# A hybrid SSD and latent-attention step: the query projection turned round, with tables for the rotation

## The chip, the cores and the metric

The kernel runs on one core of one Trainium2 chip. The metric is the time of one execution on the device in microseconds. A core has five engines that run side by side: TensorE (PE in the profile, with its weight loads listed apart as PEld), VectorE (DVE), ScalarE (ACT), GpSimd (POOL) and SyncE (SP), which here issues most DMA transfers. PE multiplies a stationary operand (up to 128x128, loaded first) with a moving one (up to 512 columns) and writes to PSUM, which DVE and ACT read; the other operands lie in SBUF, 128 partitions wide. DRAM is reached by DMA.

## The reference

One step of a two-layer decoder trunk: a Mamba-2 layer, then a multi-head latent attention layer (MLA), each added to the residual, and a final norm. There are 1024 prompt tokens and 64 sample tokens (8 sequences of 8 with a paged cache of 2048 positions), 1088 in all. What matters here is how the queries come about in the MLA layer:

```python
cq = rms_norm(proj[..., :o1], q_norm_w)              # 512 wide
q = jnp.einsum('btq,qhe->bthe', cq, w_uq)            # 16 heads, 64 + 32 wide
q_nope = q[..., :MLA_QK_NOPE]
q_pe = apply_rope(q[..., MLA_QK_NOPE:], cos[:, None, :], sin[:, None, :])

def apply_rope(x, cos, sin):
    x1, x2 = xf[..., :half], xf[..., half:]          # half = 16
    return jnp.concatenate([x1 * cos - x2 * sin, x2 * cos + x1 * sin], axis=-1)
```

Each head of the prompt then attends causally to 1024 keys of width 96 (64 made from the latent by `w_uk`, 32 rotated and common to all heads). The sample tokens do it in the latent space: `q_nope` is multiplied by `w_uk` (`absorb`), and the 256 wide result meets the cached latents directly.

## The kernel before

Values are float32. A matrix product of full accuracy is made of three products: each operand is split into a high part, rounded to the type that PE multiplies fast, and a low part (`split`, L127 and L133: ACT casts, DVE subtracts), and high x high, high x low and low x high are summed in PSUM.

The order of the work on the engines: most of the kernel is written as a program and put in order for every engine ahead of time by a planner that simulates the timeline. In the head loop and the sample stage the orders of PE and POOL are as written; DVE, ACT and SP are still planned. `issue_after(x)` tells the planner to put an instruction behind x. Each engine takes its instructions strictly in its order, SP its DMAs too.

The parts that the change and the prediction touch:

- `mla_cq` (ends at L1124) makes the normed query latent of nine token tiles (eight of 128 tokens, one of 64 with the sample tokens), turned so that the latent index lies on partitions: `cqh`, `cql`, four blocks of 128 by tokens. For the sample tile the low part goes beside the high one in `cqh`, so that one matmul of 128 weight columns takes both.
- `mla_q` (L1127 to L1155) is the query projection. The columns of `w_uq` are taken in four groups c of 384 (four heads of 96), loaded and split into `wqh`, `wql` by `load_w` (L318 is its DMA). For each group, nine token tiles: the latent is stationary (128 tokens) and the weight moves (384 columns), 12 matmuls (8 for the sample tile) into one of two PSUM buffers of tag pj (L98). ACT copies the result to `qt` (L1144; `fold`, L109 and L110, for the sample tile), DVE turns the rotary part in place with four operations (L1150 to L1153) and a DMA stores 192 KB to `q_d` in DRAM, tokens by columns (L1154). So there are 36 tiles, 32 of 128 tokens.
- `layer_mla` mixes 39 early units into those 36 tiles from the tenth on: the values and keys of the first heads (`vp`, `kp`, L86), queries of heads 0 and 1 (`prep_q`) and the score maxima of head 0 (`maxpass`).
- `mla_heads` is the loop over 16 heads: in head h, 12 blocks of scores st (`qk`, L1408 to L1415), two exponentials each (L1419, L1420, once rounded and once full), their difference tl on DVE or POOL in turn (L1422), and the product with the values o (`pv`, L1439 to L1441) two blocks later. Between the blocks stand, in a fixed merge, the maxima of head h + 1 (`sc`, L1376 to L1396, with a round trip through DRAM at L1395 and L1396) and the preparation of head h + 2 (keys, values, `prep_q`).
- `prep_q(h)` (L1319 to L1358): `load_q` fetches the queries of a pair of heads with tokens on partitions, 768 KB and 48 KB (L1316, L1317), a pair ahead from the third pair on. PE then turns them: one transpose for the 64 sample tokens (L1331), two of the raw key weight of this head (L1333), all in one PSUM tile `qs`; DVE and ACT copy out `qsn` (L1336) and `wt` (L1340) and split the sample's rotary part. Then twice four transposes of 128 tokens (`qT`, L1348) and a split from PSUM into the head's `qTh`, `qTl`. Last the two matmuls of `absorb` (`ql`, L1354) and their split.

Of the kernel before, what the change touches and what calls it, by code (L numbers as in the profile page):

```python
# [8 lines left out]
F32 = mybir.dt.float32  # L9
# [8 lines left out]
SEQ = 1024  # L18
# [977 lines left out]
def mla_in(k, right, mid):  # L996
    tc, nc, I = k.tc, k.nc, k.I
    k.g_d = k.dram.tile([8, 128, T], F32, name="g_d")
    with ExitStack() as st:
        xp = st.enter_context(open_pool(tc, name="hT", bufs=1))  # L1000
        k.xh = xp.tile([128, 8, T + 64], F32R, name="hh")
        k.xl = xp.tile([128, 8, T], F32R, name="hl")

        rw = st.enter_context(open_pool(tc, name="rw", bufs=1))
        sg = ExitStack()
        wg = sg.enter_context(open_pool(tc, name="wpg", bufs=1))
        with k.h0, open_pool(tc, name="h1", bufs=1, side="right") as p0:
# [23 lines left out]
        k.cqh = hp.tile([128, 4, T + 64], F32R, name="cqh")  # L1031
        k.cql = hp.tile([128, 4, SEQ], F32R, name="cql")
# [12 lines left out]
        k.wu0 = load_w(k, wu, I["mla_w_uq"][0].rearrange("q h e -> q (h e)")[:, :384], 4, 384, "wq", 1, None, 1)  # L1045
        mla_cq(k, sp, wcq)


# [54 lines left out]
def mla_cq(k, sp, ws):  # L1103
    nc = k.nc
    for i, (t0, m) in enumerate(TILES):
# [18 lines left out]
        split(k, k.cqh[:, :, t0 : t0 + m], k.cqh[:, :, T:] if m == 64 else k.cql[:, :, t0 : t0 + m], qs[:, :, :m])  # L1124


def mla_q(k, st):  # L1127
    tc, nc, I = k.tc, k.nc, k.I
    wuq = I["mla_w_uq"][0].rearrange("q h e -> q (h e)")
    wp = st.enter_context(open_pool(tc, name="wpq", bufs=1, side="right"))  # L1130
    sp = st.enter_context(open_pool(tc, name="spq", bufs=1, side="right"))
    ct, sn = k.rope
    for c in range(4):
        cs = slice(384 * c, 384 * c + 384)
        wh, wl = load_w(k, wp if c % 2 else k.wu, wuq[:, cs], 4, 384, "wq", 1, k.wu, 1) if c else k.wu0
        for i, (t0, m) in enumerate(TILES):
            qt = sp.tile([128, 4, 96], F32, tag="qt", name=f"qt{c}{i}", bufs=2)
            qf = qt.rearrange("p h e -> p (h e)")
            p = k.psum.tile([128, 512], F32, tag="pj", name=f"pq{c}{i}", bufs=PB["pj"])
            drain(mm_tok(nc, p, m, 384, [(*both(k.cqh, k.cql, i, kk), wh[:, kk], wl[:, kk]) for kk in range(4)]))  # L1140
            if m == 64:
                fold(nc, qf, p, 384)
            else:
                nc.scalar.copy(qf[:m], p[:m, :384])  # L1144
            u = sp.tile([128, 4, 2, 16], F32, tag="u3", name=f"u3{c}{i}", bufs=2)
            w = sp.tile([128, 4, 2, 16], F32, tag="w3", name=f"w3{c}{i}", bufs=2)
            cb = bass_bcast2(ct[:m, i], 4, 2)
            sb = bass_bcast2(sn[:m, i], 4, 2)
            pe = qt[:m, :, 64:96].rearrange("p h (a e) -> p h a e", a=2)
            nc.vector.tensor_tensor(u[:m], pe, cb, op=ALU.mult)  # L1150
            nc.vector.tensor_tensor(w[:m], pe, sb, op=ALU.mult)
            nc.vector.tensor_tensor(pe[:, :, 0], u[:m, :, 0], w[:m, :, 1], op=ALU.subtract)
            nc.vector.tensor_tensor(pe[:, :, 1], u[:m, :, 1], w[:m, :, 0], op=ALU.add)  # L1153
            nc.sync.dma_start(k.q_d[t0 : t0 + m, cs], qf[:m])  # L1154
            yield  # L1155


class Heads:
    def __init__(self, k, st):
# [10 lines left out]
        self.ones_rows(0)  # L1170
        self.add_k(vp, 1)
        self.ones_rows(1)
        self.qT, self.qts = [], {}
        self.add_q(vp, 0)
        self.add_q(vp, 1)

# [131 lines left out]
                    split(k, kh[0:64, cs], kl[0:64, cs], p[64 * jj : 64 * jj + 64])  # L1308
                yield

    def load_q(self, pr):
        k, nc = self.k, self.k.nc
        qt = self.sp.tile([128, 9, 192], F32, tag="qp", name=f"qp{pr}", bufs=2 if pr else 1)
        src = k.q_d[:, 192 * pr : 192 * pr + 192]
        with k.tc.issue_after(k.lastq.ins) if pr > 1 else nullcontext():
            nc.sync.dma_start(qt[:, :8], src[:SEQ].rearrange("(i p) e -> p i e", p=128))  # L1316
            nc.sync.dma_start(qt[:64, 8], src[SEQ:])  # L1317
        self.qts[pr] = qt

    def prep_q(self, h):  # L1320
        k, nc, sp = self.k, self.k.nc, self.sp
        hg, pr, j = h // 4, h // 2, h % 2
        if j == 0 and pr < 2:
            self.load_q(pr)
        if j == 1 and 0 < pr < 7:
            self.load_q(pr + 1)
        qt = self.qts[pr]
        if h == 2:
            nc.gpsimd.memset(self.qT[2][1][96:98].bitcast(F32), 0.0)
        p = self.wt(f"qs{h}")  # L1330
        nc.tensor.transpose(p[:96, :64], qt[:64, 8, 96 * j : 96 * j + 96], k.ident[:64, :64])  # L1331
        for c in range(2):
            nc.tensor.transpose(p[:64, 128 + c * 128 : 256 + c * 128],  # L1333
                                self.wkr[:, c, 64 * (h % 4) : 64 * (h % 4) + 64], k.ident)
        qsn = sp.tile([64, 64], F32, tag="qsn", name=f"qsn{h}", bufs=2)
        nc.vector.tensor_copy(qsn, p[:64, :64])  # L1336
        qv = k.qpr[:, :, NT * h : NT * h + NT]
        split(k, qv[0:32], qv[64:96], p[64:96, :64].rearrange("p (b t) -> p b t", t=NT))
        wt = sp.tile([64, 256], F32, tag="wt", name=f"wt{h}", bufs=2)
        nc.scalar.copy(wt, p[:64, 128:384])  # L1340
        yield
        if 1 < h < 4:
            self.ones_rows(h)
        qh, ql = self.q_of(h)
        for c in range(2):
            p = self.wt(f"qT{h}{c}")
            for i in range(4):
                nc.tensor.transpose(p[:96, i * 128 : i * 128 + 128], qt[:, 4 * c + i, 96 * j : 96 * j + 96], k.ident)  # L1348
            cs = slice(512 * c, 512 * c + 512)
            split(k, qh[:96, cs], ql[:96, cs], p[:96])  # L1350
            yield
        pl = self.wt(f"ql{h}p")
        for c in range(2):
            nc.tensor.matmul(pl[:, c * 64 : c * 64 + 64], wt[:, c * 128 : c * 128 + 128], qsn,  # L1354
                             start=True, stop=True)
        src = pl[:, :128].rearrange("p (c b t) -> p c b t", c=2, t=NT)
        split(k, *(x[:, :, :, NT * h : NT * h + NT] for x in (k.qlh, k.qll)), src)
# [40 lines left out]
    def qk(self, h, qc, jb):  # L1398
# [18 lines left out]
        tl = sp.tile([128, 512], F32R, tag="tl", name="tl", bufs=3)  # L1417
        P = sp.tile([128, 512], F32, tag="P", name="P", bufs=3)
        nc.scalar.activation(th[:, :n], ps[:, :n], AF.Exp, scale=SCALE)  # L1419
        nc.scalar.activation(P[:, :n], ps[:, :n], AF.Exp, scale=SCALE)  # L1420
        eng = nc.gpsimd if jb % 2 else nc.vector
        eng.tensor_tensor(tl[:, :n], P[:, :n], th[:, :n].bitcast(F32), op=ALU.subtract)  # L1422
        return th, tl
# [553 lines left out]
def layer_mla(k):  # L1977
# [1 line left out]
    k.og_d = k.dram.tile([8, 128, SEQ], F32, name="og_d")  # L1979
    k.npool = k.I["cache_ckv"].shape[1]  # L1980
    with ExitStack() as st:
        k.q_d = k.dram.tile([T, MH * 96], F32, name="q_d")
# [40 lines left out]
def consts():  # L2023
# [10 lines left out]
    ang = (pos[:, None] * inv[None, :]).astype(np.float32).reshape(9, 128, ROPE // 2).transpose(1, 0, 2)  # L2034
    c["c_cos"] = np.ascontiguousarray(np.cos(ang))
    c["c_sin"] = np.ascontiguousarray(np.sin(ang))
    m = np.where(i[None, :] <= i[:, None], 0.0, NEG).astype(np.float32)
    c["c_maskn"] = np.ascontiguousarray(np.concatenate([m, m.T], 1))
    c["c_slot"] = (i % 32).astype(np.float32)[:, None]
# [40 lines left out]
```

## Time and profile before

| what | value |
|---|---|
| median of 3 runs (lowest, highest) | 1924.01 us (1922.32, 1925.89) |
| the profiled execution | 1926.24 us |
| its span, first to last instruction | 1924.4 us |
| mean granted clock of TensorE | 0.997 |
| query projection (first and last pq matmul of `mla_q`) | about 1222 to 1313 us |
| head loop | from there to about 1620 us |
| DMA over the span | 202.02 MB, mean 105 GB/s |

How to read the profile's rows. A group row has the line, the engine, the operation, the output and inputs by their names in the program, the shape, the count, and then busy time, mean time of one, idle time of the engine just ahead of them and what ended it. The row of one tile's view has shortest, median and longest duration of one in ns instead, and the first and last start. A row of the chain is a start, a length and the work that stood on the path to the end then. Matmuls are pipelined: the duration of one is longer than the step from one to the next, and a busy PE need not be at its peak. Lines are those of the kernel before.

### The profile page before, as it was taken

How to read it: one execution, taken by the hardware profiler on the slowest of the kernel's cores; microseconds unless marked ns; L12 is line 12 of the kernel's file. 1: busy time of each engine (PE TensorE's matmuls, PEld its weight loads, DVE VectorE, ACT ScalarE, POOL GpSimd, SP SyncE). 2: the span in 40 equal slices, each digit the busy share in tenths (PEclk: the TensorE clock that was granted, in tenths of full speed). 3: DMA queues.
4: the chain of work that ended last, by engine and by line, in shares of the span. 5: the costliest groups of instructions: out<-in, count | busy, mean ns of one | idle time of the engine just before them, and what ended most of it. 6: DMA issues, size and time to landing. Idle time of an engine off the chain costs nothing.

```text
span 1924.4 us, 33639 instructions
## 1 busy us (share of the span) xinstructions
PE 1890.9 (98%) x12023; PEld 1728.8 (90%) x12023; DVE 1206.0 (63%) x2500; ACT 1102.0 (57%) x2523; POOL 823.3 (43%) x1122
## 2 busy tenths in 40 slices
PE   8999999999999999999999999999999999899998
PEld 7999999999999999888788998998888888788887
DVE  5557676757676757665534114567877888766674
ACT  6467566667666666733214314436777777755552
POOL 2447555545654555443004222104433435774551
PEclk9999999999999999999999999999999999999999
DMA  5223323333333232645534343123111112754541
GB/s 165 53 78 91 96 79 98 86 104 86 97 83 98 85 98 81 212 152 175 164 109 129 114 163 87 63 102 96 49 47 41 52 41 60 207 185 150 156 129 39
DMA packets 181087, 202.02 MB, mean 105 GB/s; under 512 B 18828, under 2 KB 147608, under 8 KB 180536
## 3 DMA queue, kind: packets, MB, share of 16 engines
q1 hardware_dynamic: 175864, 180.08, 30.9%
q0 software_dynamic: 4976, 19.66, 3.2%
q8 instruction: 95, 1.56, 0.4%
q14 instruction: 72, 0.59, 0.1%
q10 hardware_dynamic: 80, 0.13, 0.0%
HBM read 146.52 MB, written 53.28 MB: 104 GB/s over the span
## 4 chain that ended last, share of the span: by engine, by line
PE 84%; ACT 4%; DVE 4%; DMA 4%; issue 2%; POOL 1%; SPq 0%; POOLq 0%; DVEq 0%; ACTq 0%
PE pj L86 22%; PE pz L98 7%; PE pq L98 6%; PE pob L98 5%; PE p L98 5%; PE poa L98 3%; PE py L637 2%; PE sc L86 2%; PE o L86 2%; PE sc L1376 2%; PE o L1439 2%; PE o L1441 2%; PE st L1408 2%; PE st L1409 2%; PE st L1410 2%
## 5 line engine op out<-in xcount | busy, mean ns | idle before, releaser
L86 PE MATMUL pj<-xl,wih 128*128 128x384 f32 (+1 forms) x768 | 255.4, 333 | 0.0
L86 PE MATMUL pj<-xh,wih 128*128 128x384 f32 (+1 forms) x768 | 252.9, 333 | 1.2 <-ACT xh L273 0.9
L86 PE MATMUL pj<-xh,wil 128*128 128x384 f32 (+1 forms) x768 | 252.9, 329 | 0.0
L1422 POOL TENSOR_TENSOR tl<-P,th 128x384 fp32r<-128x384 f32 (+1 forms) x96 | 90.5, 942 | 234.3 <-ACT P L1420 192.7
L525 DVE SCALAR_TENSOR_TENSOR acc<-raw,vec,acc 128x1112 f32<-128x1112 f32 x96 | 140.9, 1469 | 14.9 <-ACT acc L521 14.0
L86 PEld LDWEIGHTS pj<-xh,wih 128*128 128x128 f32 x768 | 143.8, 188 | 2.6 <-ACT xh L273 1.4
L86 PEld LDWEIGHTS pj<-xl,wih 128*128 128x128 f32 x768 | 144.5, 188 | 1.0
L86 PEld LDWEIGHTS pj<-xh,wil 128*128 128x128 f32 x768 | 144.5, 188 | 0.5
L98 PE MATMUL pz<-wih,xh 128*128 128x256 f32 x504 | 143.2, 288 | 1.2 <-ACT z L566 1.2
L98 PE MATMUL pz<-wil,xh 128*128 128x256 f32 (+1 forms) x504 | 139.7, 283 | 0.0
L1419 ACT ACTIVATE th<-st 128x512 fp32r<-128x512 f32 x192 | 94.8, 494 | 66.7 <-PE st L1415 51.0
L98 PE MATMUL pz<-wih,xl 128*128 128x256 f32 x448 | 128.5, 287 | 0.0
L632 ACT ACTIVATE M<-M,tok 128x128 f32<-128x128 f32 (+1 forms) x288 | 90.8, 388 | 58.5 <-DVE M L628 58.1
L1712 POOL TENSOR_TENSOR kvl<-pgr,kvh 128x256 fp32r<-128x256 f32 x128 | 97.3, 787 | 57.0 <-ACT kvh L1710 52.6
L133 DVE TENSOR_TENSOR wil<-wraw,wih 128x512 fp32r<-128x512 f32 x88 | 73.9, 845 | 39.6 <-ACT wih L127 33.6
L98 PEld LDWEIGHTS pz<-wih,xh 128*128 128x128 f32 x504 | 95.9, 190 | 2.2 <-ACT z L566 1.7
L1420 ACT ACTIVATE P<-st 128x512 f32<-128x512 f32 x192 | 93.8, 489 | 0.0
L98 PEld LDWEIGHTS pz<-wil,xh 128*128 128x128 f32 (+1 forms) x504 | 92.8, 184 | 0.1
L1422 DVE TENSOR_TENSOR tl<-P,th 128x512 fp32r<-128x512 f32 x96 | 74.3, 774 | 19.6 <-ACT P L1420 19.5
L98 PEld LDWEIGHTS pz<-wih,xl 128*128 128x128 f32 x448 | 85.3, 190 | 0.7
L613 POOL TENSOR_TENSOR xdd<-xsT,tok 128x256 f32<-128x256 f32 x64 | 48.7, 761 | 86.8 <-ACT xsT L599 83.9
L127 ACT CAST wih<-wraw 128x512 fp32r<-128x512 f32 x92 | 56.1, 618 | 44.9 <-PE pj L86 29.4
(833 smaller groups left out, 6274.6 us busy)
## 6 DMA issues: line engine op xcount, KB each, us to landing
wraw<-in_ssd_w_in SPq DMA_DIRECT2D x92, 256.0 KB
M<-acs_d SPq DMA_DIRECT2D x64, 256.0 KB
s<-in_state_ssm SPq DMA_DIRECT2D x32, 256.0 KB
y_d<-y SPq DMA_DIRECT2D x64, 128.0 KB
out_s_ssm<-s SPq DMA_DIRECT2D x32, 256.0 KB
q_d<-qt SPq DMA_DIRECT2D x32, 192.0 KB
qp<-q_d SPq DMA_DIRECT2D x8, 768.0 KB
wraw<-in_ssd_w_out SPq DMA_DIRECT2D x10, 512.0 KB
```

Of the source, the lines that this page charges most:

```text
L86: nc.tensor.matmul(out, a, b, start=(i == 0), stop=(i == n - 1))
L98: nc.tensor.matmul(o, a, b, start=(j == 0), stop=(j == len(ops) - 1))
L127: k.cast = nc.scalar.copy(hi, src)
L133: return (eng or nc.vector).tensor_tensor(lo, src, hi.bitcast(F32), op=ALU.subtract)
L525: last = nc.vector.scalar_tensor_tensor(acc, raw[:, j : j + n], k.convw[j][:, blk : blk + 1], acc, op0=ALU.mult, op1=ALU.add)
L613: nc.gpsimd.tensor_tensor(v3(xdd), v3(xsT), hb(2), op=ALU.mult)
L632: nc.scalar.activation(M[:m, h, :m], M[:m, h, :m], AF.Exp, bias=tk[:, 0, 4 * g + h : 4 * g + h + 1])
L637: nc.tensor.matmul(py[:m, h * 64 : h * 64 + 64], M[:m, h, :m], xsT[:m, h * 64 : h * 64 + 64], start=True, stop=True)
L1419: nc.scalar.activation(th[:, :n], ps[:, :n], AF.Exp, scale=SCALE)
L1420: nc.scalar.activation(P[:, :n], ps[:, :n], AF.Exp, scale=SCALE)
L1422: eng.tensor_tensor(tl[:, :n], P[:, :n], th[:, :n].bitcast(F32), op=ALU.subtract)
L1712: nc.gpsimd.tensor_tensor(rl[:, j], raw[:, j], rh[:, j].bitcast(F32), op=ALU.subtract)
```

## The change

The query projection is turned round, so that its result has the query's index on partitions and tokens in the columns; what the heads got by transposes they now load.

- The host lays `w_uq` out anew: each group c of four heads has its 384 columns in three blocks of 128: the 64-wide parts of heads 0 and 1, those of heads 2 and 3, and the rotary parts, first all 16-wide first halves, then all second halves. A new input `mla_w_ukt` holds `w_uk` per head already turned, 64 by 256.
- `mla_q` takes, for each group c, the three blocks b against three column groups of tokens (384, 384 and 320): nine pieces x, each of 12 matmuls with the weight block stationary and the latent moving. In group 0 the blocks change fastest (b = x mod 3), in the others the token groups do (b = x div 3), so that the three rotary pieces come last there.
- For b < 2 ACT copies the piece to `qt` and a DMA stores it to `qn_d`. For b = 2 DVE multiplies it from PSUM by a cosine table into u, and the two halves crosswise by a sine table (with signs) into w, POOL adds u and w into `qt`, and a DMA stores it to `qr_d`. The two tables, 128 by 1088, are new inputs, loaded at the head of `mla_q`. u and w have one buffer each.
- `load_q` fetches one head, 96 partitions by 1088 tokens, with three DMAs, one head ahead from head 3 on. `prep_q` has no transposes: it loads `wt` (64 KB), splits the sample's rotary part and the two halves of the head's queries straight from `qt` in SBUF, and gives `qt` itself to the matmuls of `absorb`. These splits are put behind the latest full exponential.
- The low part of the latent's sample tile goes to `cql` like the others.

```diff
+def load_wq(k, pool, c):
+    raw = load_raw(k.wu, 4, 384, 1)
+    k.nc.sync.dma_start(raw, k.I["mla_w_uq"][c])
+    w = [pool.tile([128, 4, 384], F32R, tag="wq" + x, name=f"wq{x}{c}", bufs=1) for x in "hl"]
+    split(k, *w, raw)
+    return w
 def mla_q(k, st):
-    ct, sn = k.rope
+    ct = sp.tile([128, T], F32, name="cosq")
+    sn = sp.tile([128, T], F32, name="sinq")
+    nc.sync.dma_start(ct, I["c_cosq"])
+    nc.sync.dma_start(sn, I["c_sinq"])
     for c in range(4):
-        for i, (t0, m) in enumerate(TILES):
-            drain(mm_tok(nc, p, m, 384, [(*both(k.cqh, k.cql, i, kk), wh[:, kk], wl[:, kk]) for kk in range(4)]))
...
-            nc.vector.tensor_tensor(u[:m], pe, cb, op=ALU.mult)
-            nc.vector.tensor_tensor(w[:m], pe, sb, op=ALU.mult)
-            nc.vector.tensor_tensor(pe[:, :, 0], u[:m, :, 0], w[:m, :, 1], op=ALU.subtract)
-            nc.vector.tensor_tensor(pe[:, :, 1], u[:m, :, 1], w[:m, :, 0], op=ALU.add)
-            nc.sync.dma_start(k.q_d[t0 : t0 + m, cs], qf[:m])
+        wh, wl = load_wq(k, wp if c % 2 else k.wu, c) if c else k.wu0
+        for x in range(9):
+            b, ci = (x % 3, x // 3) if c == 0 else (x // 3, x % 3)
+            t0, n = TG[ci]
+            ts, bs = slice(t0, t0 + n), slice(128 * b, 128 * b + 128)
+            p = k.psum.tile([128, 512], F32, tag="pj", name=f"pq{c}{x}", bufs=PB["pj"])[:, :n]
+            mm3(nc, p, [y for kk in range(4) for y in ((wh[:, kk, bs], k.cqh[:, kk, ts]), (wh[:, kk, bs], k.cql[:, kk, ts]),
+                                                      (wl[:, kk, bs], k.cqh[:, kk, ts]))])
+            qt = sp.tile([128, 384], F32, tag="qt", name=f"qt{c}{x}", bufs=2)[:, :n]
+            if b < 2:
+                nc.scalar.copy(qt, p)
+                nc.sync.dma_start(k.qn_d[2 * c + b][:, ts], qt)
             else:
-                nc.scalar.copy(qf[:m], p[:m, :384])
+                u, w = (sp.tile([128, 384], F32, tag=y + "3", name=f"{y}3{c}{x}", bufs=1)[:, :n] for y in "uw")
+                nc.vector.tensor_tensor(u, p, ct[:, ts], op=ALU.mult)
+                nc.vector.tensor_tensor(w[:64], p[64:], sn[:64, ts], op=ALU.mult)
+                nc.vector.tensor_tensor(w[64:], p[:64], sn[64:, ts], op=ALU.mult)
+                nc.gpsimd.tensor_tensor(qt, u, w, op=ALU.add)
+                nc.sync.dma_start(k.qr_d[c][:, ts], qt)
-    def load_q(self, pr):
+    def load_q(self, h):
+        qt = self.sp.tile([96, T], F32, tag="qp", name=f"qp{h}", bufs=2)
+        hh = 16 * (h % 4)
+        with k.tc.issue_after(k.lastq.ins) if h > 2 else nullcontext():
+            nc.sync.dma_start(qt[0:64], k.qn_d[h // 2][64 * (h % 2) : 64 * (h % 2) + 64])
+            for a in range(2):
+                nc.sync.dma_start(qt[64 + 16 * a : 80 + 16 * a], k.qr_d[h // 4][64 * a + hh : 64 * a + hh + 16])
     def prep_q(self, h):
+        if h < 3:
+            self.load_q(h)
+        if 1 < h < MH - 1:
+            self.load_q(h + 1)
-        nc.tensor.transpose(p[:96, :64], qt[:64, 8, 96 * j : 96 * j + 96], k.ident[:64, :64])
-        for c in range(2):
-            nc.tensor.transpose(p[:64, 128 + c * 128 : 256 + c * 128],
-                                self.wkr[:, c, 64 * (h % 4) : 64 * (h % 4) + 64], k.ident)
-        nc.vector.tensor_copy(qsn, p[:64, :64])
-        nc.scalar.copy(wt, p[:64, 128:384])
+        nc.sync.dma_start(wt, k.I["mla_w_ukt"][h])
+        with k.tc.issue_after(self.expi.ins) if self.expi else nullcontext():
+            split(k, qv[0:32], qv[64:96], qt[64:96, SEQ:].rearrange("p (b t) -> p b t", t=NT))
         yield
         for c in range(2):
-            for i in range(4):
-                nc.tensor.transpose(p[:96, i * 128 : i * 128 + 128], qt[:, 4 * c + i, 96 * j : 96 * j + 96], k.ident)
-            split(k, qh[:96, cs], ql[:96, cs], p[:96])
+            with k.tc.issue_after(self.expi.ins) if self.expi else nullcontext():
+                split(k, qh[:96, cs], ql[:96, cs], qt[:, cs])
             yield
-            nc.tensor.matmul(pl[:, c * 64 : c * 64 + 64], wt[:, c * 128 : c * 128 + 128], qsn,
+            nc.tensor.matmul(pl[:, c * 64 : c * 64 + 64], wt[:, c * 128 : c * 128 + 128], qt[:64, SEQ:],
                              start=True, stop=True)
```

More of the change, by code (lines that the diff above doesn't have):

```diff
@@ L1030, in mla_in @@
         hp = mid.enter_context(open_pool(tc, name="hp", bufs=1, side="right"))
-        k.cqh = hp.tile([128, 4, T + 64], F32R, name="cqh")
-        k.cql = hp.tile([128, 4, SEQ], F32R, name="cql")
+        k.cqh = hp.tile([128, 4, T], F32R, name="cqh")
+        k.cql = hp.tile([128, 4, T], F32R, name="cql")
         sp = mid.enter_context(open_pool(tc, name="sp2", bufs=1, side="right"))
@@ L1044, in mla_in @@
         k.wu = wu
[L1045 removed]
+        k.wu0 = load_wq(k, wu, 0)
         mla_cq(k, sp, wcq)
@@ L1123, in mla_cq @@
         nc.vector.tensor_tensor(qs[:, :, :m], pv, k.qn.unsqueeze(2).to_broadcast([128, 4, m]), op=ALU.mult)
-        split(k, k.cqh[:, :, t0 : t0 + m], k.cqh[:, :, T:] if m == 64 else k.cql[:, :, t0 : t0 + m], qs[:, :, :m])
+        split(k, k.cqh[:, :, t0 : t0 + m], k.cql[:, :, t0 : t0 + m], qs[:, :, :m])
+def load_wq(k, pool, c):
[4 more added lines that the diff above has]
+    return w
@@ L1309, in prep_kv @@
                 yield
-    def load_q(self, pr):
+    def load_q(self, h):
         k, nc = self.k, self.k.nc
[L1313 to L1318, printed above, removed]
+        qt = self.sp.tile([96, T], F32, tag="qp", name=f"qp{h}", bufs=2)
[4 more added lines that the diff above has]
+                nc.sync.dma_start(qt[64 + 16 * a : 80 + 16 * a], k.qr_d[h // 4][64 * a + hh : 64 * a + hh + 16])
+        self.qts[h] = qt
@@ L1320, in prep_q @@
     def prep_q(self, h):
         k, nc, sp = self.k, self.k.nc, self.sp
[L1322 to L1327, printed above, removed]
+        if h < 3:
+            self.load_q(h)
+        if 1 < h < MH - 1:
+            self.load_q(h + 1)
+        qt = self.qts.pop(h)
         if h == 2:
             nc.gpsimd.memset(self.qT[2][1][96:98].bitcast(F32), 0.0)
-        p = self.wt(f"qs{h}")
@@ L1331, in prep_q @@
-        nc.tensor.transpose(p[:96, :64], qt[:64, 8, 96 * j : 96 * j + 96], k.ident[:64, :64])
-        for c in range(2):
-            nc.tensor.transpose(p[:64, 128 + c * 128 : 256 + c * 128],
-                                self.wkr[:, c, 64 * (h % 4) : 64 * (h % 4) + 64], k.ident)
-        qsn = sp.tile([64, 64], F32, tag="qsn", name=f"qsn{h}", bufs=2)
-        nc.vector.tensor_copy(qsn, p[:64, :64])
+        wt = sp.tile([64, 256], F32, tag="wt", name=f"wt{h}", bufs=2)
+        nc.sync.dma_start(wt, k.I["mla_w_ukt"][h])
@@ L1981, in layer_mla @@
     with ExitStack() as st:
-        k.q_d = k.dram.tile([T, MH * 96], F32, name="q_d")
+        k.qn_d = k.dram.tile([MH // 2, 128, T], F32, name="qn_d")
+        k.qr_d = k.dram.tile([MH // 4, 128, T], F32, name="qr_d")
         PB.update(PB2)
@@ L2036, in consts @@
     c["c_sin"] = np.ascontiguousarray(np.sin(ang))
+    angq = (pos[:T, None] * inv[None, :]).astype(np.float32).T
+    c["c_cosq"] = np.ascontiguousarray(np.tile(np.cos(angq), (8, 1)))
+    c["c_sinq"] = np.ascontiguousarray(np.tile(np.sin(angq), (8, 1)) * np.repeat(np.float32([-1, 1]), 64)[:, None])
     m = np.where(i[None, :] <= i[:, None], 0.0, NEG).astype(np.float32)
@@ L2069 @@
     given = {n: np.ascontiguousarray(inputs[n]) for n in _INS}
+    w = inputs["mla_w_uq"][0].reshape(4, 128, 4, 4, 96)
+    w = np.concatenate([w[..., a:b].reshape(4, 128, 4, -1) for a, b in ((0, 64), (64, 80), (80, 96))], 3)
+    given["mla_w_uq"] = np.ascontiguousarray(w.transpose(2, 1, 0, 3))
+    given["mla_w_ukt"] = np.ascontiguousarray(inputs["mla_w_uk"][0].transpose(1, 2, 0))
     given.update(consts())
```

20 lines of the change are left out of this document (2 added, 18 removed).

## The prediction

> **What bounds the kernel now.** I read the page first, for the share of each engine and the chain that ended last.
>
> ```profile
> PE 1890.9 (98%) x12023; PEld 1728.8 (90%) x12023; DVE 1206.0 (63%) x2500; ACT 1102.0 (57%) x2523; POOL 823.3 (43%) x1122
> ...
> PE 84%; ACT 4%; DVE 4%; DMA 4%; issue 2%; POOL 1%; SPq 0%; POOLq 0%; DVEq 0%; ACTq 0%
> ```
>
> TensorE (PE) carries 84% of the chain. But an average says nothing of the stage that is edited, so next come stretches: the start of the query projection, the rest of it, and the head loop.
>
> ```profile
> core 0: us, PE busy (x) PEld busy (x) DVE busy (x) ACT busy (x) POOL busy (x), PEclk, DMA share, GB/s
> 1222.00:1248.00 26.00, 26.00 (x164) 25.40 (x163) 16.58 (x55) 11.73 (x24) 7.21 (x8) 1.00 0.28 97
> 1248.00:1314.00 66.00, 65.77 (x379) 62.56 (x378) 41.49 (x156) 23.33 (x49) 0.00 (x0) 1.00 0.30 105
> 1314.00:1600.00 286.00, 285.42 (x1666) 245.63 (x1665) 229.51 (x577) 217.16 (x493) 118.62 (x116) 1.00 0.19 50
> ```
>
> The granted clock is 1.00 throughout. DVE is busy 80% of the head loop (229.51 of 286) and ACT 76%: high, but below PE. A busy PE may still be a stalled one, so third come the waits inside the loop (1330 to 1590 us): who waited for whom, microseconds in total, times, longest.
>
> ```profile
> ACT th L1419 <- PE st L1415: 35.7, 49, 1.2
> ...
> PEld o L1441 <- DVE tl L1422: 1.9, 5, 0.4
> ```
>
> ACT waits for PE; the largest wait of PE's weight loads is 1.9 us in 260. So PE is the bound of the projection and of the loop, and work that leaves PE there leaves the span.
>
> **The transposes.** The change takes every query transpose (L1331, L1348) and every key-weight transpose (L1333) from PE. Counts with the shortest, median and longest duration in ns, then what they take on the chain (start, length, what):
>
> ```profile
> L1348 PE MATMUL qT<-ident,qp x128: 270/272/284, 1261.4 to 1605.9; 128*96 128x128 f32 x128
> ```
>
> ```profile
> L1333 PE MATMUL qs<-ident,w x32: 272/286/301, 1259.0 to 1597.2; 128*64 128x128 f32 x32
> ```
>
> ```profile
> 1298.53 14.07 PE pq L98 x80
> ...
> 1314.11 1.46 PE kp L86 x6
> ...
> 1321.86 0.19 PE qs L1331
> 1322.05 0.34 PE qs L1333 x2
> ...
> 1325.28 0.44 PE qT L1348 x4
> ```
>
> There are 128 + 16 + 32 = 176 transposes. Four take 0.44 us, not 4 x 0.272, since matmuls are pipelined and a single duration is longer than the step to the next. A head has one qs group (0.19 + 0.34) and two qT groups (0.88): 1.41 us. Sixteen heads: **-22.6 us**, of which 2.8 are the two heads prepared inside the projection and 19.7 the fourteen prepared in the loop.
>
> The Trainium skill's page "TensorE: Matmul & The Clock Gate", Part 4, gives a PE transpose about 275 ns in a kernel's context. The 272 ns rows agree as durations; used as cost per instruction, 176 x 0.275 would make an estimated 48 us. The chain's 0.44 us for four decides, and the sum does not use the page.
>
> **The projection's matmuls.**
>
> ```profile
> L98 PE MATMUL pq<-wqh,cqh 128*128 128x384 f32 x144 | 49.1, 343 | 0.2 <-ACT qt L1144 0.2
> L98 PE MATMUL pq<-wql,cqh 128*128 128x384 f32 (+1 forms) x144 | 48.1, 338 | 0.0
> L98 PE MATMUL pq<-wqh,cql 128*128 128x384 f32 x128 | 43.3, 338 | 0.0
> ```
>
> Before: 144 + 144 + 128 = 416 of 384 columns. The chain steps 14.07 / 80 = 0.176 us each; 512 columns step 1.46 / 6 = 0.243, so the step follows the columns closely and 320 should take 320 / 384 of 0.176, 0.147. After: 36 groups of 12, two thirds with 384 columns and one third with 320: 288 x 0.176 + 144 x 0.147 = 71.9 against 416 x 0.176 = 73.2. **-1.3 us**. The sample tile no longer needs a matmul of its own.
>
> **The rotation.** Before, each of 36 tiles had an ACT copy and four short DVE operations; now a third of the tiles have three long DVE operations straight from PSUM and one POOL addition. The rows nearest to the new ones: DVE on 64x384 from PSUM, POOL on 128x384.
>
> ```profile
> L110 DVE TENSOR_TENSOR qt<-qt,pq x4: 540/543/547, 1246.8 to 1313.2; 64x384 f32<-64x384 f32 x4
> ```
>
> ```profile
> L1422 POOL TENSOR_TENSOR tl<-P,th 128x384 fp32r<-128x384 f32 x24 | 24.2, 1008 | 60.7 <-ACT P L1420 40.0 <-PE o L1441 20.6
> ```
>
> DVE then has 12 x 3 x 0.543 = 20 us in place of 144 short operations. Hidden under PE, that counts as nothing either way, and so do the ACT copies saved. What counts is a chain: u and w have one buffer each, so the next rotated tile starts after the addition, 3 x 0.543 + 1.01 = 2.64 us, while PE makes a tile in 2.11 (or 1.76) and has two PSUM buffers. In weight groups 1 to 3 the three rotated tiles stand in a row. With the first ready at 0, the second frees its buffer at 4.27 and the third at 6.91; PE wants them at 3.87 and 6.38: 0.4 + 0.5 us lost per row. Two rows: 1.9. The third runs into the loop, where the last bank comes free 3.0 us after the last matmul, and the first kp follows 1.5 us after it today: 0 to 1.5, I take 0.7. **+2.6 us**, bounds 0 (other work lies between the tiles) and 7.8 (12 tiles, 2.64 against a mean 1.99). Group 0 deals them every third tile: nothing.
>
> **Loads.** Two tables of 544 KB are new, at the head of the projection, and the first rotated tile is its third. Rows: issues on SP's queue, sizes, the wait of that load's reader, the copy of the third tile today.
>
> ```profile
> 1315.82 0.58 SPq L1316 DMA_DIRECT2D qp<-q_d  x1
> 1316.45 0.58 SPq L1317 DMA_DIRECT2D qp<-q_d  x1
> ```
>
> ```profile
> qp<-q_d SPq DMA_DIRECT2D x8, 768.0 KB
> ```
>
> ```profile
> PEld qs L1331 <- DMA qp<-q_d: 0.4, 1, 0.4
> ```
>
> ```profile
> 1222.64 0.34 SPq L1188 DMA_DIRECT2D mk<-in_c_maskn  x1
> ```
>
> ```profile
> 1230.14 0.48 ACT L1144 COPY qt<-pq 128x384 f32<-128x384 f32 x1
> ```
>
> The transpose at 1321.86 waited for these 768 KB and the 48 KB of the sample rows, issued from 1315.82: 6.0 us. At that rate the tables take 8.0 us. Issued with the mask at 1222.6 they land near 1231 where 1230.1 is wanted; the weights behind them move back too. From 0 to 8.0 us; nearest to the wanted time, **+1.0 us**.
>
> A head now has four small loads in place of its half of a pair's two. Query loads keep a head's lead. Head 2 has none in the loop: its 408 KB takes 3 us at that rate, from about 1316, before 1322: nothing. The key weight (64 KB) is loaded where the transposes were, and PE's ql matmul waits for it, with st and o matmuls behind in a written order.
>
> ```profile
> 1375.07 0.34 PE qs L1333 x2
> ...
> 1379.09 0.58 PE ql4p L1354 x4
> ```
>
> ```profile
> 1298.87 0.28 SPq L1395 DMA_DIRECT2D nd<-nr  x1
> ...
> 1300.90 0.26 SPq L1396 DMA_DIRECT2D qTh<-nd  x1
> ```
>
> The first pair shows the cover at its shortest (head 4): 4.0 us. The second bounds a small transfer: a 4 KB write let the read that needs it go after 2.0 us; the 816 KB load took 6.0. So 0 to 2 us in each of four heads; 64 KB is nearest the small one: 0. SP issues some 50 DMAs more at up to 0.58 us, 29 us over 390: hidden, unless the round trip of the maxima (L1395, L1396) queues behind. ACT's query cast now waits for a DMA; behind it stand the exponentials, then tl, then PE's o. A head of lead hides it.
>
> **Shorter covers.** With 1.41 us less PE per head, the path st, two exponentials, tl, o (two steps of lead) is tighter. It costs 2 us now; I add as much again, **+2.0**, bounds 0 and 19.7. The dropped ACT copy (wt) and DVE copy (qsn) ease it.
>
> Sum: -22.6 - 1.3 + 2.6 + 1.0 + 2.0 = **-18.3 us**. The profiled execution took 1926.24 us (span and 1.8 around it), so 1907.9 by its own time; the median shown, 1924.01, lies 2.2 lower: **1905.7, I say 1906**.
>
> **Rivals.**
> A, *the loop is bound by ACT and DVE*: PE would idle at o for tl. For: 80% and 76% busy, rising to 85% and 80% at a loop 19.7 us shorter. Against: 2 us of waits now. Half the loop's gain lost, 9.9 instead of 2.0: 1913.6; all: 1923.4.
> B, *the projection waits* for tables and rotation at their upper bounds: 8.0 + 7.8 instead of 3.6, 1917.9. For: three tiles in a row. Against: POOL is idle there (0.00) and DVE loses work.
> C, *slower*: the query splits on DVE read two SBUF operands now (before, one was in PSUM) and queue against POOL's tl.
>
> ```profile
> L1422 DVE TENSOR_TENSOR tl<-P,th 128x512 fp32r<-128x512 f32 x48 | 39.1, 815 | 13.5 <-ACT P L1420 13.5
> ...
> L133 DVE TENSOR_TENSOR qTl<-qT,qTh 96x512 fp32r<-96x512 f32 x24 | 16.4, 682 | 3.2 <-ACT qTh L127 2.9
> ```
>
> If each of 28 splits in the loop held PE for a POOL operation of 1.01 us, 28.2 us: 1933.9. It decides from 18.3 / 28 = 0.65 us per split. Against: DVE's two-SBUF form shows 815 ns where the PSUM form shows 682, 0.13 apiece and off PE. The Trainium skill, "SBUF — State Buffer", Who interferes with whom, has this as an exclusive lock in which the later one fully blocks; the 0.13 shows that it bites, but seldom.
> D, *nothing moves*: the transposes filled slots that PE would idle through. Against: the chain passes through them. 1924.
>
> **Chances.** Forecast (1900 to 1911) 0.62; A 0.14; B 0.11; C 0.09; D 0.04. The range 1900 to 1919 leaves out C, D and the top of A: about 0.16. This kernel's measurement tells 0.2% (3.8 us) from no change. Faster: forecast, B and nearly all of A, 0.86; same: D and the end of A, 0.05; slower 0.09.
>
> **What would show it.** Loop: a head takes 1.3 to 1.4 us less, PE's waits for tl stay under 5 us in all; above 10 is A. Projection: 12 matmuls still step 2.11 us, with gaps under 1 us at the rotated rows; DVE waiting for tables above 2 us is B. DVE splits of queries over 1.3 us with o waiting are C. A gain that isn't near 1.4 per head makes the first term wrong.

## The result and the profile after

The changed kernel takes **1936.9 us** (median of 3 runs, 1936.23 to 1940.28) against 1924.01 before: a ratio of 1.0068, 95% interval 1.0046 to 1.009. It is slower, where 1906 was forecast.

The page of the kernel after, engine rows:

```profile
PE 1881.5 (97%) x11863; PEld 1718.6 (89%) x11863; DVE 1211.6 (63%) x2372; ACT 1090.7 (56%) x2495; POOL 851.0 (44%) x1134
```

PE lost 160 instructions and 9 us of work, DVE lost 128 instructions and gained 6 us: its instructions became longer. Where the time went is read from two marks that both kernels have, the `absorb` matmuls of heads 2 and 15 (the view of one tile; first start is what counts). Before:

```profile
L1354 PE MATMUL ql2p<-qsn,wt x4: 272/272/320, 1332.8 to 1333.2; 64*128 64x64 f32 x4
...
L1354 PE MATMUL ql15p<-qsn,wt x4: 272/272/320, 1611.1 to 1611.5; 64*128 64x64 f32 x4
```

After, with the first matmul of the query projection (1222.5 before):

```profile
L86 PE MATMUL pq<-cqh,wqh x144: 307/336/446, 1220.7 to 1312.2; 128*128 128x384 f32 x96, 128*128 128x320 f32 x48
...
L1354 PE MATMUL ql2p<-qp,wt x4: 272/272/320, 1333.0 to 1333.4; 64*128 64x64 f32 x4
...
L1354 PE MATMUL ql15p<-qp,wt x4: 272/272/320, 1619.9 to 1620.3; 64*128 64x64 f32 x4
```

| stretch, us | before | forecast | after |
|---|---|---|---|
| projection, first pq to ql2 | 110.3 | 108.4 | 112.3 |
| head loop, ql2 to ql15 (13 heads prepared) | 278.3 | 262.0 | 286.9 |

The forecast column is the prediction's own: 110.3 - 2.8 - 1.4 (head 2) - 1.3 + 2.6 + 1.0, and 278.3 - 13 x 1.41 + 2.0. So 24.9 us are missing in the loop and 3.9 in the projection. In the loop, the stretches of the kernel after:

```profile
core 0: us, PE busy (x) PEld busy (x) DVE busy (x) ACT busy (x) POOL busy (x), PEclk, DMA share, GB/s
1350.00:1400.00 50.00, 47.51 (x279) 41.27 (x278) 42.51 (x98) 36.24 (x83) 20.78 (x20) 1.00 0.21 55
...
1450.00:1500.00 50.00, 47.68 (x245) 41.19 (x244) 36.94 (x85) 34.80 (x78) 17.14 (x16) 0.90 0.20 53
1500.00:1550.00 50.00, 48.33 (x273) 41.45 (x272) 41.63 (x99) 37.07 (x84) 21.50 (x19) 0.97 0.15 40
1550.00:1600.00 50.00, 47.20 (x244) 39.58 (x244) 40.58 (x90) 36.44 (x81) 20.37 (x18) 0.97 0.20 52
```

PE now idles 1.7 to 2.8 us of every 50 (the row left out has 1.65 and a clock of 1.00), and the granted clock falls below 1.00 in three of the five stretches. It waits for DVE and POOL (waits, 1330 to 1590 us, total, times, longest):

```profile
PEld o L1441 <- POOL tl L1422: 10.0, 10, 1.5
...
PEld nmp L1391 <- DVE nm L1388: 6.8, 8, 1.5
...
PEld o L1441 <- DVE tl L1422: 3.0, 6, 1.1
```

With 1.3 more at st, 21.1 us together; before, 3.6. The groups of the same window say why. First the kernel after; the kTl row is the control, a subtraction that still reads one operand from PSUM:

```profile
L1452 POOL TENSOR_TENSOR og<-og,rl 64x512 f32<-64x512 f32 x23 | 33.6, 1461 | 31.8 <-DVE og L1450 20.2 <-ACT P L1420 6.1 <-PE o L1441 2.8
...
L1422 POOL TENSOR_TENSOR tl<-P,th 128x384 fp32r<-128x384 f32 x24 | 27.3, 1137 | 60.0 <-ACT P L1420 40.8 <-PE st L1415 19.2
...
L133 DVE TENSOR_TENSOR qTl<-qp,qTh 96x512 fp32r<-96x512 f32 x24 | 24.0, 1010 | 0.2
...
L133 DVE TENSOR_TENSOR kTl<-kp,kTh 64x512 fp32r<-64x512 f32 x22 | 15.1, 686 | 2.4 <-ACT kTh L127 2.1
...
L133 DVE TENSOR_TENSOR qpr<-qp,qpr 32x64 fp32r<-32x64 f32 x11 | 8.4, 766 | 2.3 <-ACT qpr L127 1.9
```

Then two rows of the kernel before:

```profile
L1452 POOL TENSOR_TENSOR og<-og,rl 64x512 f32<-64x512 f32 x24 | 32.0, 1334 | 29.5 <-ACT rl L1451 14.2 <-DVE og L1450 9.1 <-PE sc L1376 4.6
...
L133 DVE TENSOR_TENSOR qpr<-qs,qpr 32x64 fp32r<-32x64 f32 x12 | 2.7, 222 | 0.4
```

The query's low part took 682 ns with one operand in PSUM and takes 1010 with both in SBUF; the sample's, 222 and 766; the key's, untouched, 686 and 686. POOL's own operations grew too (1334 to 1461, 1008 to 1137). Of the 24 splits of the queries in this window of the kernel after, 8 ran with POOL idle and took 0.68 us on average; 16 ran beside an instruction of POOL and took 1.18. One instance, in the timeline of the kernel after (start, length); DVE:

```profile
1416.90 2.29 DVE L133 TENSOR_TENSOR qTl<-qp,qTh 96x512 fp32r<-96x512 f32 x1
1419.12 0.61 DVE L1381 CUSTOM_DVE_ANT_0 sc<-sc,mk,mx 128x384 f32<-128x384 f32 x1
...
1419.65 0.96 DVE L1422 TENSOR_TENSOR tl<-P,th 128x512 fp32r<-128x512 f32 x1
...
1421.14 0.67 DVE L133 TENSOR_TENSOR qTl<-qp,qTh 96x512 fp32r<-96x512 f32 x1
```

POOL and PE at the same time:

```profile
1415.47 1.94 POOL L1452 TENSOR_TENSOR og<-og,rl 64x512 f32<-64x512 f32 x1 [1.21 <-ACT rl L1451]
1417.37 2.69 POOL L1422 TENSOR_TENSOR tl<-P,th 128x512 fp32r<-128x512 f32 x2
```

```profile
1418.69 0.50 PE L1441 MATMUL o<-tl,Vh 128*128 128x512 f32 x1 [0.58 <-POOL tl L1422]
```

The split lasts 2.29 us while POOL runs og and tl; the next one, at 1421.14 with POOL idle, 0.67. Behind the long one DVE's maximum and its tl start late; POOL's og takes 1.94, the tl behind it starts late, and PE waits for it. Before, the same split beside a POOL tl of 1.28 us took its usual time:

```profile
1415.63 0.68 DVE L133 TENSOR_TENSOR qTl<-qT,qTh 96x512 fp32r<-96x512 f32 x1
```

```profile
1415.12 1.28 POOL L1422 TENSOR_TENSOR tl<-P,th 128x512 fp32r<-128x512 f32 x1
```

### The profile page after: what moved, and what is told of

Read it like the earlier page. It is cut to its first block, busy times and chain, and to the rows that moved or that the text cites. A ratio compares the mean times of both kernels' runs of the same rounds, so it can differ in the third digit from the quotient of the medians.

```text
span 1935.1 us, 33244 instructions
## 1 busy us (share of the span) xinstructions
PE 1881.5 (97%) x11863; PEld 1718.6 (89%) x11863; DVE 1211.6 (63%) x2372; ACT 1090.7 (56%) x2495; POOL 851.0 (44%) x1134
## 5 line engine op out<-in xcount | busy, mean ns | idle before, releaser
L1422 POOL TENSOR_TENSOR tl<-P,th 128x384 fp32r<-128x384 f32 (+1 forms) x96 | 95.5, 997 | 141.8 <-ACT P L1420 103.0
L632 ACT ACTIVATE M<-M,tok 128x128 f32<-128x128 f32 (+1 forms) x288 | 90.4, 387 | 53.6 <-DVE M L628 53.4
L1441 PE MATMUL o<-tl,Vh 128*128 128x512 f32 x192 | 70.6, 368 | 10.9 <-POOL tl L1422 7.8
```

The lines of the kernel that those rows point to most:

```text
L632: nc.scalar.activation(M[:m, h, :m], M[:m, h, :m], AF.Exp, bias=tk[:, 0, 4 * g + h : 4 * g + h + 1])
L1441: nc.tensor.matmul(po[:, o:], va, tl[:, :n], start=False, stop=(jb == nj - 1))
```

## The experiments

Two theories for the loop. **L**: a DVE subtraction with both operands in SBUF can't overlap POOL's reads of SBUF; the two hold each other up, tl and the maxima come late, and PE idles. This is the prediction's rival C. **O**: the splits stand badly in DVE's and ACT's orders, because they are put behind the latest full exponential. For the projection, the suspects are the two buffers of `qt`, which wait for their stores, and the row of three rotated pieces.

**1. The kernel before, with only the operand moved.** The transposes and the sample's split stay; the query's low part is taken from two SBUF operands.

```diff
-            split(k, qh[:96, cs], ql[:96, cs], p[:96])
+            nc.scalar.copy(qh[:96, cs], p[:96])
+            src = qh[:96, cs].bitcast(F32) if h > 1 else p[:96]
+            nc.vector.tensor_tensor(ql[:96, cs], src, qh[:96, cs].bitcast(F32), op=ALU.subtract)
```

> The kernel before, with one edit: from head 2 on, the DVE subtraction that makes the low part of a head's queries reads two SBUF operands (the high part twice, so the low part is zero and the queries are less exact) in place of one in PSUM and one in SBUF. Transposes, loads and order stay. Theory L (the DVE subtraction with two SBUF operands queues against POOL's work): its mean goes from 682 ns to about 1000 and the time rises to 1929 to 1944 us. Rivals O (the order behind the exponentials) and W (late loads): nothing of theirs is changed, so 1924 within 4 us and 682 ns.

Measured: 1931.35 us, ratio to before 1.0028 (1.0015 to 1.0041); the loop 283.2, 4.9 longer. Its group and waits:

```profile
L1352 DVE TENSOR_TENSOR qTl<-qTh 96x512 fp32r<-96x512 f32 x22 | 27.4, 1246 | 2.7 <-ACT qTh L1350 2.7
```

```profile
PEld o L1443 <- DVE tl L1424: 5.1, 8, 0.8
...
PEld nmp L1393 <- DVE nm L1390: 3.7, 7, 0.6
```

Moving one operand from PSUM to SBUF takes the instruction from 682 to 1246 ns and makes the kernel slower, with nothing else in the program changed. The waits rise by 5.2 us, as much as the loop.

**2. The kernel after, with only the operand moved back.** One matmul per split fills a PSUM tile, from which DVE subtracts. The tile holds other data, so this kernel leaves out the true low parts.

```diff
-                split(k, qh[:96, cs], ql[:96, cs], qt[:, cs])
+                nc.scalar.copy(qh[:96, cs], qt[:, cs])
+                src = qt[:, cs]
+                if h > 1:
+                    p = self.wt(f"qT{h}{c}")
+                    nc.tensor.matmul(p[:96], self.identr[:, :96], k.kvh[:, 0, cs], start=True, stop=True)
+                    src = p[:96]
+                nc.vector.tensor_tensor(ql[:96, cs], src, qh[:96, cs].bitcast(F32), op=ALU.subtract)
```

(The sample's 64 columns likewise.)

> The kernel after, with one edit: from head 2 on, the low parts of the queries and of the sample's rotary part are taken from a PSUM tile that one matmul fills with other data (so the low parts are wrong); loads, order and casts stay. It adds some 0.6 us of PE to a head, 8 us in all. L: DVE's subtraction returns to about 680 ns, waits of o for tl shrink, and the time falls to 1913 to 1921 us. O and W: what they blame is unchanged, 1937 to 1945.

Measured: 1921.16 us, 0.9966 (0.9952 to 0.998): faster than before, although PE does 39 matmuls more in the loop than in the kernel after. The loop is 272.3, 14.6 shorter than after.

```profile
L1363 DVE TENSOR_TENSOR qTl<-qT,qTh 96x512 fp32r<-96x512 f32 x25 | 17.0, 679 | 0.5 <-ACT qTh L1357 0.4
...
L1348 DVE TENSOR_TENSOR qpr<-qs,qpr 32x64 fp32r<-32x64 f32 x12 | 2.7, 222 | 2.1 <-ACT qpr L1343 1.5
```

Both splits are back at their old durations. With the casts, loads and order rule of the kernel after in place, only the source of DVE's operand decides. L holds.

**3. The low part on POOL** instead of DVE.

```diff
-                split(k, qh[:96, cs], ql[:96, cs], qt[:, cs])
+                split(k, qh[:96, cs], ql[:96, cs], qt[:, cs], nc.gpsimd if h > 1 else None)
```

> The kernel after, but from head 2 on POOL makes the low parts of the head's queries (28 subtractions of 96x512) instead of DVE; the sample's rotary low parts stay on DVE. L says the harm is DVE standing behind POOL with everything queued on DVE (maxima, tl, og): then DVE is freed of 28 x 1.0 us, but POOL takes 28 x 1.4 us in its written order, with its tl behind: 1922 to 1937 us, PE's waits for POOL's tl rise and those for nm and DVE's tl fall. If the port does not matter: 1937 or more, since POOL is the slower engine for it.

Measured: 1940.9 us, 1.0074 (1.0055 to 1.0094): no better than after. That is above the 1922 to 1937 of L and inside the band of its rival (1937 or more). One of the ten runs took 1926.14 us at a mean clock of 0.996, the others 1937.4 to 1944.05 at 0.986 to 0.992, so a part of the time is lost clock. The rows tell more:

```profile
L1422 DVE TENSOR_TENSOR tl<-P,th 128x512 fp32r<-128x512 f32 x46 | 43.9, 955 | 9.2 <-ACT P L1420 8.9
...
L133 POOL TENSOR_TENSOR qTl<-qp,qTh 96x512 fp32r<-96x512 f32 x24 | 31.3, 1302 | 3.7 <-ACT qTh L127 3.6
...
L1422 DVE TENSOR_TENSOR tl<-P,th 128x256 fp32r<-128x256 f32 x24 | 19.7, 822 | 0.1
```

Now DVE's tl, also a subtraction of two SBUF operands, pays: 808 to 955 ns and 520 to 822 against the kernel after. So the rows speak for L as to the cause, though the time does not: L had priced this version too low. As far as these two kernels show, what counts is that two-SBUF work overlaps on the two engines at all, and hardly which of them does the split.

**4. The order rule dropped** for the 28 large splits.

```diff
-            with k.tc.issue_after(self.expi.ins) if self.expi else nullcontext():
+            with nullcontext():
                 split(k, qh[:96, cs], ql[:96, cs], qt[:, cs])
```

> The kernel after without the rule that puts the splits of prep_q behind the latest full exponential; the planner is free to order them. O: the time falls by 10 us or more, to 1927 or below. L: the subtractions still read two SBUF operands next to POOL, so the time stays at 1933 to 1941 with the mean still near 1000 ns.

Measured: 1947.83 us, 1.0104 (1.008 to 1.0129), slower than after. O falls: the rule helps. L's number was missed as well, by 7 us. Against the kernel after, the stretch up to ql of head 2 grows from 112.3 to 116.7 us and the loop from 286.9 to 293.0. In the loop, the waits are 3.3 us more and the lost clock 2.0 (table below). Grown or new among the waits are:

```profile
PEld st L1408 <- ACT P L1420: 6.7, 10, 1.4
...
PEld sc L1376 <- DVE mx L1381: 4.3, 3, 2.0
```

The split is shorter (761 ns, where L had expected about 1000), but now ACT's cast for it often stands ahead of the exponentials, and PE waits for those: the three longest waits of the first row (1.16 to 1.39 us) come right behind such a cast.

**5. Four buffers for `qt`** (`bufs=2` to `bufs=4`), and **6. the same with the blocks dealt** in every group, so that a rotated piece is each third one.

```diff
-            b, ci = (x % 3, x // 3) if c == 0 else (x // 3, x % 3)
+            b, ci = (x % 3, x // 3)
```

> The kernel after with four buffers for qt in the projection instead of two. If the projection's loss (about 6 us of PE stalls there) is the wait of ACT and POOL for the stores of qt, it ends some 5 us earlier: 1931 to 1933. If it is the chain u, w, addition, with one buffer each: 1936 to 1938. L says nothing of it, and the head loop stays as long.

> The kernel after with four buffers for qt and the rotary pieces every third in all groups. Against the kernel with four buffers alone (ql of head 2 at 1331.3 us in its trace, 1333.0 after): if the row of three costs, ql of head 2 comes 2 to 4 us earlier and the time is 1928 to 1932; if not, it is within 1 us of it. The loop keeps its locks: 280 us or more.

Measured: 1933.88 us, 1.0051 (1.0033 to 1.0069), and 1933.17 us, 1.0039 (1.0025 to 1.0053). Total times say little here; the projection stretch does: 112.3 after, 110.5 with four buffers (1331.3 less 1220.8), 108.8 dealt (1327.6 less 1218.8). Read so, the store waits cost 1.8 us, not the 5 that were expected, and the rows of three 1.7. But neither size is shown. Experiments 2 and 4 run the same instructions in the same order in the projection as the kernel after, and yet the time from the first to the last start of a pq matmul is 90.3 and 90.4 us there, against 91.8 after and 90.2 with four buffers. (The mark itself moved by 3.7 from the fifth to the sixth kernel, but 2.0 of that lie ahead of the projection, where the two do not differ.) That both waits exist, the chain of the kernel after shows, one behind the other:

```profile
1292.42 1.03 POOL qt L1161
...
1293.47 1.84 DMA qr_d<-qt
...
1295.40 0.49 ACT qt L1154
...
1295.91 4.04 DMA qn_d<-qt
...
1300.06 0.49 ACT qt L1154
```

A rotated piece ends late, its store ends later, and only then does ACT get a buffer for a piece that has waited in PSUM.

The pair tells one thing more. In the loop the two programs are the same, and PE's idle time of the five stretches is too (10.84 and 10.97 us of 250). Yet the loop took 281.0 us in one trace and 286.9 in the other. The fifth had a clock of 1.00, 1.00, 1.00, 1.00, 0.97; the sixth 1.00, 1.00, 0.90, 0.97, 0.97. Lost clock (a row's share missing, times 50 us) is 1.5 against 8.0 us, a difference of 6.5 for the 5.9 measured.

**7 to 9. Split once, in the projection,** where the result is still in PSUM, and let the heads load high and low parts.

```diff
-                nc.scalar.copy(qt, p)
-                nc.sync.dma_start(k.qn_d[2 * c + b][:, ts], qt)
+                split(k, *hl, p)
+                for y, d in zip(hl, k.qn_d):
+                    nc.sync.dma_start(d[2 * c + b][:, ts], y.bitcast(F32))
...
-                nc.gpsimd.tensor_tensor(qt, u, w, op=ALU.add)
-                nc.sync.dma_start(k.qr_d[c][:, ts], qt)
+                nc.gpsimd.tensor_tensor(u, u, w, op=ALU.add)
+                split(k, *hl, u)
+                for y, d in zip(hl, k.qr_d):
+                    nc.sync.dma_start(d[c][:, ts], y.bitcast(F32))
...
-            with k.tc.issue_after(self.expi.ins) if self.expi else nullcontext():
-                split(k, qh[:96, cs], ql[:96, cs], qt[:, cs])
```

The eighth deals the blocks as the sixth does; the ninth besides gives the split of the rotated pieces to POOL and loads heads 0 and 1 earlier.

```diff
-                split(k, *hl, u)
+                nc.gpsimd.tensor_copy(hl[0], u)
+                nc.gpsimd.tensor_tensor(hl[1], u, hl[0].bitcast(F32), op=ALU.subtract)
...
+            if n == 9:
+                hd.load_q(0)
+                hd.load_q(1)
```

> The kernel after with the queries split once, in the projection: ACT and DVE make high and low parts straight from PSUM (rotary pieces from u), both are stored, and a head loads both parts straight into the tiles that PE reads, at the head of its preparation; the sample's parts too. No split of queries is left in the head loop; the numbers computed are the same. L: DVE loses 28 x 1.0 and 14 x 0.77 us, ACT some 25 us; the loop (ql of head 2 to ql of head 15, 286.9 us after, 278.3 before) falls to 262 to 268 and the time to 1911 to 1920 us, the projection costing 0 to 5 us for twice the stores. W (late loads hold the loop): twice the bytes per head make it worse, above 1937.

> The former with the rotary pieces every third in all four weight groups, not three in a row in groups 1 to 3. If the row of three holds PE in the projection (0.4 + 0.5 us a row and up to 1.5 at its end were forecast), it is 2 to 4 us faster than the former; if the stores hold it, the same within 1.5 us. The loop stays as it is.

> The kernel with dealt rotary pieces and the split in the projection, with two edits there: POOL, idle in the projection, casts and subtracts the rotary pieces (so that ACT does not stand behind the addition in its order), and the loads of heads 0 and 1 are written right behind the first weight group instead of at their preparation (PE waited 3.6 and 3.9 us for one of them). In the former trace ql of head 2 came at 1343.8 us (1332.8 before) and the loop was 264 us. L: the loop stays at 262 to 266 us; if those two waits were what the projection lost, ql of head 2 comes at 1330 to 1338 and the time is 1906 to 1915 us, faster than both kernels. If twice the stores hold the projection, it stays at 1917 to 1922.

Measured: 1930.47 us, 1.0028 (1.0016 to 1.0039); 1919.21, 0.9968 (0.9953 to 0.9983); **1915.14, 0.9949 (0.9933 to 0.9965)**, faster than both kernels. The loop takes 264.2, 264.0 and 263.8 us: the gain that was expected there (262 to 268). What differs is the projection: 130.8, 121.9 and 113.6 us. The seventh missed its time, 1911 to 1920, since the projection cost 18.5 us more than after in place of 0 to 5; dealing brought 11.3 us where 2 to 4 were expected; the ninth lies at the upper edge of its 1906 to 1915. In the seventh and eighth, ACT's queue, taken in order, holds the rotated pieces' casts, which wait for POOL's sum, and the plain pieces stand behind them. A row of the eighth's waits in the projection:

```profile
ACT qh L127 <- POOL u L1166: 39.2, 11, 5.6
```

In the ninth this wait is gone, since POOL makes those casts itself. The ninth also loads heads 0 and 1 earlier, and no run separates the two edits. The waits in the ninth's loop:

```profile
PEld o L1445 <- POOL tl L1426: 5.3, 13, 0.9
...
PEld o L1445 <- DVE tl L1426: 1.8, 1, 1.8
```

Do waits and clock account for the loop? To 278.3 before, take off 18.3 for the transposes where they are gone, add the matmuls of experiment 2 (26 of 512 columns at 0.243), the waits of PE's weight loads for o, nmp, st and sc (rows of 0.5 us and more) over the 3.6 of before, and the lost clock of the five stretches of 50 us from 1350 to 1600 us:

| kernel | waits, us | lost clock, us | worked out | measured loop |
|---|---|---|---|---|
| 1, before with SBUF operand | 8.8 | 0 | 283.5 | 283.2 |
| after | 21.1 | 8.0 | 285.5 | 286.9 |
| 2, after with PSUM operand | 8.5 | 0 | 271.2 | 272.3 |
| 3, low part on POOL | 24.1 | 7.0 | 287.5 | 286.7 |
| 4, order rule dropped | 24.4 | 10.0 | 290.8 | 293.0 |
| 5, four buffers | 21.6 | 1.5 | 279.5 | 281.0 |
| 6, dealt | 21.7 | 8.0 | 286.1 | 286.9 |
| 9, split in the projection | 9.5 | 0 | 265.9 | 263.8 |

All eight agree within 2.3 us (waits and clock are read over 250 to 260 us of the loop), and no term was fitted. The seventh and the eighth, whose loops start later, have waits of 9.3 us (1352 to 1612 us) and 9.2 (1345 to 1605) and no lost clock: 265.7 and 265.6 worked out, 264.2 and 264.0 measured.

## Why the prediction was wrong

The step that failed is **"Shorter covers"**, +2.0 us, together with the reason given against **rival C**: "DVE's two-SBUF form shows 815 ns where the PSUM form shows 682, 0.13 apiece and off PE". In its place the runs put 17.5 us of waits and 8.0 of lost clock, of 26.9 that the loop takes beyond the 260.0 of the transposes alone. The waits lie inside the bounds that were given for that term, 0 to 19.7; it was the 2.0 that was wrong. The lost clock had no term at all: the prediction read 1.00 in the kernel before and took it over without a reason. By these figures the loop would take an estimated 278.9 us at full clock, as long as before: the waits used up what the transposes gave, and the lost clock (with 2.0 us in the projection) made the profiled execution slower than before.

- *The row was the wrong witness.* 815 ns, the mean of tl, mixes two cases, and the trace of before shows both. Of the 48 such subtractions in its window (128x512, 1330 to 1590 us) 31 ran with POOL idle and took 0.69 us on average; 17 ran beside an instruction of POOL and took 1.05, five of them 1.76. Here is the spread (with the shorter tl of 256 columns), then one of the five and POOL's instruction at that time:

```profile
L1422 DVE TENSOR_TENSOR tl<-P,th x72: 406/691/1767, 1329.6 to 1587.3; 128x512 fp32r<-128x512 f32 x48, 128x256 fp32r<-128x256 f32 x24
```

```profile
1392.10 1.76 DVE L1422 TENSOR_TENSOR tl<-P,th 128x512 fp32r<-128x512 f32 x1
```

```profile
1392.02 1.28 POOL L1452 TENSOR_TENSOR og<-og,rl 64x512 f32<-64x512 f32 x1 [1.61 <-ACT rl L1451]
```

The splits overlap POOL far more often: in the same trace 18 of 24 ran beside it, at 0.68 us like the other six, since one operand lay in PSUM. So the price for overlap stood in the trace of before, and the mean hid it: "it bites, but seldom" was true of tl and not of the splits. With both operands in SBUF a split cost 0.33 us more on average (1010 against 682), the sample's 0.54 more (766 against 222), and a single one up to 1.6 more.

- *"Off PE" was wrong.* DVE had no slack to hide it. In the kernel after it is 85% busy between 1350 and 1400 us (42.51 of 50), and behind a split stand a maximum and a tl that PE asks for next. Experiment 1, in which the transposes and the sample's split stay and no rule binds the order, moves the same operand for only 4.9 us; which of these differences makes it cheaper was not separated.
- *Rival C* had the mechanism and nearly the price (28.2 us, 1933.9), with too small a chance. The Trainium skill, "SBUF — State Buffer", Who interferes with whom, says that a DVE instruction with two SBUF inputs contends with one of GpSimd that reads SBUF, and that one with a single SBUF input does not. The trace agrees on both counts: 1010 beside 682, and kTl at 686 in both kernels. It also says that the order of issue decides who blocks; here both grew, POOL's og from 1334 to 1461 ns.
- *The range* left out C on the strength of the same mean, and so held neither the time nor any slower one.

What held:

- *The transposes' worth.* Where the contention is gone the loop is 14.1 to 14.5 us shorter (experiments 7 to 9) in spite of 5.9 more of waits in the ninth. The 18.3 forecast for 13 heads at 1.41 us lies between the 14.5 and the 20.4 that these figures give without and with the waits.
- *The matmuls.* 24 of them, half of 384 and half of 320 columns, were put at 12 x 0.176 + 12 x 0.147 = 3.88 us; the chain of the kernel after has

```profile
1281.42 3.89 PE pq L86 x24
```

- *The rotation.* The two rows below were put at 543 and 1010 ns. The rows of three cost about 1.7 us as read above (2.6 forecast); the wait of `qt` for its stores was not foreseen.

```profile
L1158 DVE TENSOR_TENSOR u<-pq,cosq x12: 486/558/560, 1227.6 to 1314.9; 128x384 f32<-128x384 f32 x8, 128x320 f32<-128x320 f32 x4
```

```profile
1289.56 1.01 POOL qt L1161
```

- *The tables* cost nothing: no wait for them is among the projection's waits (+1.0 forecast, inside its bounds).
- *Rival A*, the loop bound by ACT and DVE, names the right engine, but not for its reason: experiment 2 does the same work on DVE, and more on PE, at 272.3 us. The sign that was given for A, waits for tl above 10 us, was met in the kernel after (10.0 + 3.0), and so was that of C, splits of over 1.3 us (5 of 24, the longest 2.29). The first sign does not tell the two apart.

**Open.** Even dealt and with four buffers the projection takes 108.8 us where the sum without the rotation's and the tables' terms gives 104.8; these 4 us were not separated. Nor is it settled why the clock falls, and why in one execution and not in another of the same loop.

## What to carry to other kernels

Removing a transpose also removes its PSUM tile, and with it the side from which the next instruction reads. Before counting such an instruction as "the same work", look at where each of its operands now lies and what POOL does at that moment; a mean over instances that mostly run with POOL idle is no price for those that run beside it, so look at the two apart. If the value must be split, split it once at its source, while it is still in PSUM, and load the halves.

## What the hardware showed that was not expected

**The clock falls in pieces.** Two ten-microsecond stretches of the kernel after:

```profile
1460.00:1470.00 10.00, 8.76 (x47) 7.43 (x46) 9.05 (x19) 6.85 (x17) 1.67 (x2) 0.97 0.17 48
1470.00:1480.00 10.00, 10.00 (x37) 9.18 (x37) 5.07 (x16) 4.20 (x11) 2.73 (x3) 0.52 0.28 70
```

The same two in experiment 5, whose loop is the same program:

```profile
1460.00:1470.00 10.00, 8.77 (x55) 7.75 (x53) 8.56 (x22) 6.96 (x17) 1.66 (x2) 1.00 0.08 21
1470.00:1480.00 10.00, 10.00 (x53) 8.48 (x53) 9.07 (x21) 9.21 (x21) 5.39 (x5) 1.00 0.29 72
```

After 1.2 us of idle PE, one execution ran the next ten microseconds at a granted clock of 0.52 and the other at 1.00 (37 and 53 matmuls). The spread of experiment 5 goes with it: 1929.2 us at a mean clock of 0.995, 1940.24 at 0.989. The Trainium skill, "TensorE: Matmul & The Clock Gate", A second HAM failure mode: psum-queue depth-cycling, tells of a kernel whose many short idles made the clock swing between half and full. The 0.52 fits it; the longest wait of PE's weight loads in this loop was 1.5 us. Over all the kernels of this case, stretches below 1.00 between 1350 and 1600 us are found only where PE idles 10.8 us or more of these 250 (after, experiments 3 to 6), and none where it idles 3.7 or less (before, 1, 2, 7 to 9). That short idles bring the clock down is thus likely and not shown. In the kernel after, PE idled 4% of the loop (10.9 of 250 us), and the clock took 8.0 us more.
